# Bias tables kept once in DRAM and read with reversed keys, and a residual rescaled by VectorE: a change to a two-block transformer kernel

## The chip, the cores and the metric

The kernel runs on one core of a Trainium2 chip. A core has a TensorE (matmul; its weight loads are listed apart as PEld), a VectorE (DVE), a ScalarE (ACT), a GpSimd (POOL) and a SyncE (SP), which here only issues DMAs. All DMAs of the core, from SP's queue and from GpSimd's, run on the same 16 DMA engines. The metric is the device time of one execution in microseconds; lower is better.

## What is computed

One sequence of 256 tokens with 2048 features goes through two transformer blocks in fp32. Cut to what matters here:

```python
# block 1: NSA attention (16 heads, 4 key groups) and a SwiGLU feed-forward
h = x + nsa_mixer(rmsnorm(x, mix_norm_g), rel_bias, ...)
h = h + swiglu(rmsnorm(h, ffn_norm_g), ffn_w_in, ffn_w_out)
x = rmsnorm(h, final_norm_g)

# block 2: modulation from c, two attentions side by side, a squared-ReLU feed-forward
mod = silu(c) @ w_mod + b_mod            # six vectors of 2048
h = rmsnorm(x, attn_norm_g) * (1 + sc1) + sh1
proj = h @ w_in
o_a = swa_sink_attention(q_a, k_a, v_a, sinks, rel_bias_2)   # 16 heads, window of 128
o_b = mla_attention(q_nope, q_rope, k_nope, k_rope, v_b)     # 8 heads
x = x + g1 * (concat(o_a, o_b) @ w_out)
h = rmsnorm(x, mlp_norm_g) * (1 + sc2) + sh2
x = x + g2 * (relu(h @ w_ff1) ** 2 @ w_ff2)
out = rmsnorm(x, final_norm_g_2)
```

NSA and SWA add a relative bias to their scores: `bias[q, k] = rel_bias[bucket(q - k)]`, which depends only on the distance of query and key, and places outside the causal window are masked.

## The kernel before

**Products.** Activations lie feature-major, [128 features, 256 tokens]. A weight matrix streams through SBUF in pieces of 512 KB: SP's queue loads `raw` (5 buffers), ScalarE rounds it to a high part `whi` (line 84), VectorE subtracts for the low part `wlo` (line 85), each with 4 buffers, and TensorE makes three products of each tile (lines 127 to 129, or 163 to 165 where tokens are the output rows). So each piece of 512 KB gives TensorE 24 products of 256 columns.

**Order.** Each engine works through a queue of its own in order. The program is traced once, and a scheduler sets the order in each queue. Background work is spread over the products by `step`: in block 1 the stream over w_mod (`mod_columns`: GpSimd's queue loads 512 KB, line 705; VectorE multiplies and adds, line 711; after 16 loads TensorE sums over the lanes, line 692), and before it the loads for the compression of keys and values (line 479, GpSimd's queue, 256 KB each, two for each piece while the second key gemm runs). `after` holds such a load back until the last product traced before it. The compression's products (line 497) need `ku`, which VectorE makes (line 470) from `kc`, the evacuated key and value products (line 395).

**Bias.** `bias_table` makes a table [16 heads, 384 distances] on TensorE and VectorE (lines 354 and 356) and GpSimd's queue writes it to a DRAM scratch 128 times over, once for each of 128 query rows (line 358: 3 MB out of the 16 partitions of `btab`). It is called twice: for NSA at the start of `nsa`, for SWA ahead of the loop over the four NSA head groups. `bias_rows` (line 362) reads from it, each partition q from its own copy with an offset of one element more for each q, so that row q holds the biases of its 256 keys in ascending order. NSA does this once for each group of four heads (512 KB), SWA once for each pair of heads (256 KB), both with two buffers. `soft` then adds scores and bias, takes the row's extremum (line 540, VectorE), and ScalarE makes the exponentials (line 542).

**Block 2's attention** (`block2_attention`). `h` holds the input of block 1's last norm until the end of `qgroup(0)`. Then its square sums give `r1`, `r1s` holds `r1` on every partition, and GpSimd multiplies `h` in place by `r1s` and by `vecs["final"]`: four times two operations on [128, 4 x 256] (lines 816 and 817). Then come the MLA latents, and a loop: `mla_pair(2 * i)` and `swa(i)` for i in 0 to 3, with `qgroup(4)` after the first, then `swa(4)` to `swa(7)`. An MLA pair multiplies the queries up, applies the rope (`rope`, lines 899 to 903: a product with `swap`, then three VectorE operations, the last of which reads two tiles in SBUF), and then runs two heads (scores in lines 909 to 912). The next reader of `h` is the first evacuation of `mlp` (line 1034).

Of the kernel before, what the change touches and what calls it, by code (L numbers as in the profile page):

```python
# [17 lines left out]
S = 256  # L18
# [20 lines left out]
def constants():  # L39
    f = np.float32  # L40
    ident = np.eye(128, dtype=f)
    dist = 255 - np.arange(384)
# [24 lines left out]
class Kernel:  # L67
# [8 lines left out]
    # ---------------------------------------------------------------- helpers  # L76
# [19 lines left out]
    def load_w(self, pieces, kk, n):  # L96
        """pieces: (dest column, AP) ; returns the high and low part [128, kk, n]."""
        return self.split_w(self.load_raw(pieces, kk, n), kk, n)
# [16 lines left out]
    def raw_cols(self, w, ld, row, kk, cols):  # L115
        """cols: list of (first column, count)"""
        n = sum(c for _, c in cols)
        pieces, o = [], 0
        for c0, cn in cols:
            pieces.append((lambda t, o=o, cn=cn: t[:, :, o:o + cn],  # L120
                           self.src(w, row * ld + c0, [[ld, 128], [128 * ld, kk], [1, cn]])))
            o += cn
        return self.load_raw(pieces, kk, n)
# [7 lines left out]
    def gemm(self, w, ld, row, xs, cols, evac, kk=2, order=None):  # L131
        """out^T[cols, S] = w[row:, cols]^T x ; evac(i, bank) gets two output tiles a bank;
        order: that of the contraction, in pieces of kk"""
# [19 lines left out]
    def gemm_tok(self, w, ld, row, xs, cols, evac, kk=2, lag=0):  # L153
        """out[S, cols] = x^T w[row:, cols] ; evac(token tile, bank)
        lag: by how many pieces of the contraction the second token tile follows the first"""
# [36 lines left out]
    def step(self, units):  # L192
        """advances the background streams by the tensor engine's time (1: 16 x 512 weight rows/columns)"""
# [6 lines left out]
    def columns(self, specs, tag, queue=None):  # L200
        """specs: (AP of a vector, rows of 128) -> [128, rows] with one column for each row of 128"""
# [16 lines left out]
    def rstd_col(self, terms, eps, pool, name):  # L218
        """terms: list of ([128 features, S] AP, column [128,1]) whose weighted sum over features
        is the mean square; returns the column [128 tokens, 2] of 1/sqrt(mean + eps)."""  # L220
# [11 lines left out]
    def sqrt_table(self):  # L232
        """has the table of the square root loaded ahead of its use"""
        self.nc.scalar.activation(self.warm, self.sacc[:, 0:1], AF.Sqrt)

    def rsqrt(self, v, pool, name, n=2):
        """1/sqrt of a column, with a Newton step after the table's square root"""
# [10 lines left out]
    def replicate(self, col, n=2):  # L248
        """[128 tokens, 2] column -> psum [128, S], the same row on every partition"""
# [31 lines left out]
    # ---------------------------------------------------------------- start  # L281
    def start(self):
# [5 lines left out]
        # opens the tensor engine's clock gate while the first loads run  # L288
# [11 lines left out]
    def norm_x(self):  # L300
        """x into feature-major h, x * g split in parts; the sums of squares follow in self.inner"""
# [42 lines left out]
    # ---------------------------------------------------------------- NSA  # L344
    def bias_table(self, rel, which, pool):
        """table[h, 255 - dist] = -bias, masked places BIG, in a DRAM scratch once for each of 128 rows"""
# [10 lines left out]
        d = self.dram.tile([128, 16, 384], F32, name=f"bt{which}")  # L357
        nc.gpsimd.dma_start(d.rearrange("q h i -> h q i"), t[:, None, :].to_broadcast([16, 128, 384]))
        return d

    def bias_rows(self, d, h0, n, dst):
        self.nc.gpsimd.dma_start(dst, bass.AP(tensor=d.tensor, offset=d.offset + h0 * 384 + 127,
                                              ap=[[16 * 384 - 1, 128], [384, n], [1, 256]]))

    def nsa(self, xs, ssq, mp):
        nc, a, tc = self.nc, self.a, self.tc
        W, LD = a["nsa_w_in"], 5168
        with ExitStack() as es:
# [3 lines left out]
            # keys of a group: selected, window of the first token tile, compressed; the second tile's  # L372
# [92 lines left out]
    def blocks(self, ku, kc, pos, ci):  # L465
        """the overlapping blocks with their positions added, one row of the block after another"""
# [8 lines left out]
    def load_w1(self, j):  # L475
        """rows 256 (j // 2) .. of the first matrix of one of the compressions"""
# [13 lines left out]
    def compress(self, cp, ku, kT, vcc):  # L490
        """both compressions, side by side in two halves of the array's columns"""
# [42 lines left out]
    def soft(self, parts, sb, sums, sh=None):  # L534
        """parts: (psum slice, bias slice, columns of sb, mask column count): the scores and bias are
        negated; leaves exp(s - max) in sb and the sums in `sums`"""
# [8 lines left out]
    def nsa_head(self, w, hd, g, q, bt, kT, vt, vcc, gate):  # L545
# [6 lines left out]
        # first token tile, and the compressed scores of both  # L552
# [7 lines left out]
        self.soft([(s[:, 0:128], bt[:, 128:256], sl(0, 128)), (s[:, 128:256], bt[:, 128:256], sl(128, 256)),  # L560
                   (s[:, 256:263], bt[:, 159:256:16], sl(256, 263)),
                   (s[:, 272:287], bt[:, 31:256:16], sl(272, 287))], sb, sums)
# [12 lines left out]
        # second token tile  # L575
# [6 lines left out]
        self.soft([(s[:, 0:256], bt, sl(0, 256)), (s[:, 256:512], bt, sl(256, 512))], sb, sums)  # L582
# [9 lines left out]
        # weighted values of the three branches  # L592
# [11 lines left out]
    # ---------------------------------------------------------------- residual products  # L604
    def add_h(self, ms, n=2):
        """evacuation that adds a bank's n tiles into h; ms: first tile of the first bank"""
# [7 lines left out]
    def square_sums(self, scale=None):  # L614
        """a function that adds the squares of h[k], .. h[k + n - 1], and keeps those of the last call apart"""
# [21 lines left out]
    def scaled(self, k, g):  # L637
        """h[k] * g, split"""
# [7 lines left out]
    # ---------------------------------------------------------------- first FFN  # L646
# [35 lines left out]
    # ---------------------------------------------------------------- modulation vector  # L682
    def modulation(self, pool, segs):
        """steps that stream w_mod and leave silu(c) @ w_mod of the 1024-column segments in modv"""
# [15 lines left out]
    def mod_columns(self, pool, acc, s):  # L700
        """acc = the products of silu(c) with w_mod's columns of segment s, yet to be summed over lanes"""
# [12 lines left out]
    def after(self, ins):  # L714
        """paces a background load: not before the last product traced so far"""
# [9 lines left out]
    # ---------------------------------------------------------------- second block, attention  # L725
    def block2_attention(self, es, p, vecs, mod, mv):
        """h holds the input of block 1's last norm; returns the tiles of the mixed heads"""
# [4 lines left out]
        # norms of block 1's end and of the attention's input in one factor  # L732
        r12 = self.replicate(self.rstd_col(self.sums(self.cD[:, 0:1], 1), EPS * EPS, e, "r12c"))
        xs = self.modulated(e, r12, mod["g1"], mv[:, 0:16])
        # latents
# [71 lines left out]
        # x of block 2, in place  # L807
# [6 lines left out]
        for k in range(0, KT, 4):  # L814
            hs = self.h[:, k:k + 4, :]
            nc.gpsimd.tensor_tensor(hs, hs, r1s[:, None, :].to_broadcast([128, 4, S]), OP.mult)
            nc.gpsimd.tensor_tensor(hs, hs, vecs["final"][:, k:k + 4, None].to_broadcast([128, 4, S]), OP.mult)
        # MLA latents up
# [47 lines left out]
        def swa(hp):  # L866
            bt = p.tile([128, 2, 257], F32, name="bt2", tag="bt2", bufs=2)
            self.bias_rows(d2, 2 * hp, 2, bt[:, :, 0:256])
            nc.gpsimd.tensor_copy(bt[:, :, 256], self.nsink[:, 2 * hp:2 * hp + 2])
            mix[hp] = self.swa_pair(p, qa[hp], kd[:, hp // 4, :], va, hp // 4, bt)  # L870

        for i in range(4):
            mla_pair(2 * i)
            swa(i)
# [6 lines left out]
    def modulated(self, pool, r, g, sh):  # L881
        """h * r * g + sh, split; r: the factors of the tokens on every partition"""
# [49 lines left out]
    def swa_pair(self, p, q, kd, va, g, bt):  # L932
# [3 lines left out]
        for j in range(2):  # L936
# [7 lines left out]
            self.soft([(s[:, 0:257], bt[:, j, :], cs[0]), (s[:, 257:386], bt[:, j, 128:257], cs[1])], sb, sums)  # L944
# [17 lines left out]
    # ---------------------------------------------------------------- all  # L962
# [170 lines left out]
```

## Time and profile before

| | |
|---|---|
| median of 3 runs | 2213.34 us (2207.52, 2213.34, 2214.29) |
| profiled execution, span from the first to the last instruction | 2205.4 us (no other time of this execution is given) |
| TensorE busy | 2135.2 us, 97% |
| VectorE busy | 1460.0 us, 66% |
| ScalarE busy | 1017.8 us, 46% |
| GpSimd busy | 182.2 us, 8% |
| mean granted TensorE clock | 0.984 |
| read from and written to DRAM | 487.87 MB and 8.44 MB |

How to read it: the span is that of one execution taken by the hardware profiler. Matmuls are pipelined and their ends are modelled, so a busy TensorE isn't TensorE at its peak. Granted clock is the share of full speed that the throttle allowed. In views by line, "L85 DVE wlo<-raw,whi" is line 85 of the kernel on VectorE, which writes the tile wlo from raw and whi; an arrow behind an idle time names what ended it. Views of one stretch ("56.80:92.00") give its length, then busy time and instruction count of TensorE, its weight loads, VectorE, ScalarE and GpSimd, then granted clock, DMA share and GB/s. All times are counted from the span's start.

### The profile page before, as it was taken

The page shows a single profiled execution, that of the slowest core. Times are in us where ns is not written, and L with a number is a line of the kernel's source. Part 1 is how long each engine was busy: PE and PEld are TensorE (multiplying, and loading weights), DVE is VectorE, ACT ScalarE, POOL GpSimd, SP SyncE. Part 2 cuts the span into 40 slices and gives each one's busy share as a digit, 9 for nine tenths or more (in the row PEclk, how much of TensorE's full clock was granted, in tenths as well). Part 3 has the DMA queues.
Part 4 walks back from the last instruction along what each step waited for, and adds up shares of the span by engine and source line. Part 5 has one row for each costly group of instructions (what it writes and reads, how often), then busy time and mean ns, then how long its engine had stood idle before and what let it go on. Part 6 is the DMA issues. An engine that isn't in the chain of part 4 may idle for free.

```text
span 2205.4 us, 40878 instructions
## 1 busy us (share of the span) xinstructions
PE 2135.2 (97%) x16359; PEld 2007.6 (91%) x16359; DVE 1460.0 (66%) x2113; ACT 1017.8 (46%) x1511; POOL 182.2 (8%) x321
## 2 busy tenths in 40 slices
PE   9799699999999999999999979999999999999998
PEld 8588599999999999999999978899989989988987
DVE  6356477687777777777776776567776555565555
ACT  5234356544444444443445545546534534543543
POOL 2301000000011010111010030000100000000000
PEclk9899899999999999999999999999999999999999
DMA  8969954588888888888976543367887666656754
GB/s 226 317 192 295 202 153 154 185 288 279 279 298 282 286 290 283 288 289 281 292 242 188 158 132 125 106 182 237 281 291 259 211 192 192 194 191 193 195 193 134
DMA packets 289455, 499.26 MB, mean 226 GB/s; under 512 B 22807, under 2 KB 138586, under 8 KB 289008
## 3 DMA queue, kind: packets, MB, share of 16 engines
q1 hardware_dynamic: 254480, 372.64, 53.4%
q0 software_dynamic: 34784, 124.01, 18.5%
q8 instruction: 128, 2.10, 0.4%
q14 instruction: 63, 0.52, 0.1%
HBM read 487.87 MB, written 8.44 MB: 225 GB/s over the span
## 4 chain that ended last, share of the span: by engine, by line
PE 91%; DMA 4%; DVE 2%; issue 2%; ACT 0%; POOL 0%; SPq 0%; ACTq 0%; DVEq 0%; POOLq 0%
PE acc L128 22%; PE acc L127 22%; PE acc L129 22%; PE acc L164 6%; PE acc L165 6%; PE acc L163 6%; DMA mw<-w_mod 3%; DMA raw<-nsa_w_in 1%; PE O L497 1%; DVE qr L903 1%; PE S L578 1%; DVE wlo L85 0%; PE S L939 0%; PE O L954 0%; PE O L597 0%
## 5 line engine op out<-in xcount | busy, mean ns | idle before, releaser
L84 ACT ACTIVATE whi<-raw 128x1024 fp32r<-128x1024 f32 (+1 forms) x710 | 746.6, 1052 | 975.1 <-PE acc L128 642.6
L85 DVE TENSOR_TENSOR wlo<-raw,whi 128x1024 fp32r<-128x1024 f32 (+1 forms) x710 | 854.3, 1210 | 414.3 <-ACT whi L84 400.3
L127 PE MATMUL acc<-x,whi 128*128 128x256 f32 x3200 | 889.7, 279 | 11.1 <-ACT whi L84 10.0
L128 PE MATMUL acc<-x,whi 128*128 128x256 f32 x3200 | 890.0, 279 | 0.0
L129 PE MATMUL acc<-x,wlo 128*128 128x256 f32 x3200 | 888.2, 278 | 1.6 <-DVE wlo L85 1.6
L127 PEld LDWEIGHTS acc<-x,whi 128*128 128x128 f32 x3200 | 602.7, 189 | 17.5 <-ACT whi L84 11.7
L128 PEld LDWEIGHTS acc<-x,whi 128*128 128x128 f32 x3200 | 604.3, 189 | 6.7 <-issue 5.8
L129 PEld LDWEIGHTS acc<-x,wlo 128*128 128x128 f32 x3200 | 603.7, 189 | 3.9 <-DVE wlo L85 2.3
L711 DVE SCALAR_TENSOR_TENSOR macc<-mw,csil,macc 128x1024 f32<-128x1024 f32 x180 | 231.0, 1283 | 210.8 <-DMA mw<-w_mod 210.2
L128 PE MATMUL acc<-u,whi 128*128 128x256 f32 x1260 | 352.3, 281 | 0.0
L129 PE MATMUL acc<-u,wlo 128*128 128x256 f32 x1260 | 350.1, 280 | 0.0
L127 PE MATMUL acc<-u,whi 128*128 128x256 f32 x1260 | 347.4, 280 | 1.6 <-DVE h L611 1.1
L128 PEld LDWEIGHTS acc<-u,whi 128*128 128x128 f32 x1260 | 237.4, 188 | 3.7 <-issue 2.3
L129 PEld LDWEIGHTS acc<-u,wlo 128*128 128x128 f32 x1260 | 238.3, 189 | 1.6 <-issue 0.5
L127 PEld LDWEIGHTS acc<-u,whi 128*128 128x128 f32 x1260 | 235.2, 189 | 3.2 <-issue 1.9
L164 PE MATMUL acc<-whi,u 128*128 128x512 f32 (+1 forms) x544 | 206.2, 379 | 0.0
L165 PE MATMUL acc<-wlo,u 128*128 128x512 f32 (+1 forms) x544 | 206.1, 379 | 0.0
L163 PE MATMUL acc<-whi,u 128*128 128x512 f32 (+1 forms) x544 | 204.4, 376 | 0.0
L705 POOL DMA_DIRECT2D mw<-w_mod x192 | 103.2, 538 | 959.3 <-PE acc L129 623.2
L164 PEld LDWEIGHTS acc<-whi,u 128*128 128x128 f32 x544 | 102.1, 188 | 20.6 <-issue 0.4
L163 PEld LDWEIGHTS acc<-whi,u 128*128 128x128 f32 x544 | 102.1, 188 | 20.3
L165 PEld LDWEIGHTS acc<-wlo,u 128*128 128x128 f32 x544 | 102.2, 188 | 18.4
(347 smaller groups left out, 1350.8 us busy)
## 6 DMA issues: line engine op xcount, KB each, us to landing
raw<-w_ff SPq DMA_DIRECT2D x256, 512.0 KB, 4.2
mw<-w_mod POOLq DMA_DIRECT2D x192, 512.0 KB, 5.9
raw<-ffn_w_in SPq DMA_DIRECT2D x352, 256.0 KB, 5.0
raw<-ffn_w_out SPq DMA_DIRECT2D x87, 512.0 KB, 5.2
raw<-nsa_w_in SPq DMA_DIRECT2D x82, 512.0 KB, 5.6
raw<-nsa_w_out SPq DMA_DIRECT2D x32, 512.0 KB, 4.6
raw<-w_out SPq DMA_DIRECT2D x32, 512.0 KB, 4.2
raw<-w_in SPq DMA_DIRECT2D x24, 512.0 KB, 4.0
```

The source lines that it names most:

```text
L84: self.nc.scalar.activation(hi, x, AF.Copy)
L85: self.nc.vector.tensor_tensor(lo, x, hi.bitcast(F32), OP.subtract)
L127: mm(out, wh, xh, start=first, stop=False, skip_group_check=True)
L128: mm(out, wh, xl, start=False, stop=False, skip_group_check=True)
L129: self.last = mm(out, wl, xh, start=False, stop=last, skip_group_check=True)
L163: mm(o, xt[:, 0, q], hi, start=k == 0, stop=False)
L164: mm(o, xt[:, 1, q], hi, start=False, stop=False)
L165: self.last = mm(o, xt[:, 0, q], lo, start=False, stop=k == nk - 1)
L497: nc.tensor.matmul(ph[64 * ci:64 * ci + 60, :S], ku[:, ci, 2 * n + i, :], self.w1[2 * n + ci][:, i, :], start=n + i == 0, stop=n == 15 and ...
L578: mm(s.rearrange("p (b t n) -> p t b n", t=2, n=128)[:, t], q1, kT[:, g, 272 * t:272 * t + 256].rearrange("p (b n) -> p b n", n=128), star ...
L705: ld = nc.gpsimd.dma_start(wt, self.src(self.a["w_mod_2"], k * 128 * LD + s * 1024, [[LD, 128], [1, 1024]]))
L711: nc.vector.scalar_tensor_tensor(acc, wt, csil[:, k:k + 1], acc, op0=OP.mult, op1=OP.add)
```

## The change

Three things change together.

1. `bias_table` writes its table once, [16, 384], 24 KB. So that all partitions can read from the one copy, the table is turned round: its column i stands for the distance i - 127 (before: 255 - i). Partition q starts q elements further in, and gets its 256 biases with the keys in descending order.
2. The reader goes backwards through them: `keys` builds an access pattern with a step of -1 (or -16 for the compressed keys) over the bias tile, and `soft` gets that in place of the plain slice. In SWA the sink's column moves from the end of the tile to its start.
3. The eight GpSimd operations on `h` leave. `rescale` does the same on VectorE, one operation for each of the 16 feature tiles (`h[k] * final[k] * r1s`), four of them after each of the first four MLA pairs.

```diff
 def constants():
-    dist = 255 - np.arange(384)
+    dist = np.arange(384) - 127
...
     def bias_table(self, rel, which, pool):
-        d = self.dram.tile([128, 16, 384], F32, name=f"bt{which}")
-        nc.gpsimd.dma_start(d.rearrange("q h i -> h q i"), t[:, None, :].to_broadcast([16, 128, 384]))
+        d = self.dram.tile([16, 384], F32, name=f"bt{which}")
+        nc.gpsimd.dma_start(d, t)
         return d

     def bias_rows(self, d, h0, n, dst):
-        self.nc.gpsimd.dma_start(dst, bass.AP(tensor=d.tensor, offset=d.offset + h0 * 384 + 127,
-                                              ap=[[16 * 384 - 1, 128], [384, n], [1, 256]]))
+        self.nc.gpsimd.dma_start(dst, bass.AP(tensor=d.tensor, offset=d.offset + h0 * 384,
+                                              ap=[[1, 128], [384, n], [1, 256]]))
+
+    def keys(self, t, first, last, step=1):
+        n = t.ap[-1][1]
+        return bass.AP(tensor=t.tensor, offset=t.offset + n - 1 - first,
+                       ap=[list(t.ap[0]), [-step, len(range(first, last, step))]])
...
     def nsa_head(...)
-        self.soft([(s[:, 0:128], bt[:, 128:256], sl(0, 128)), (s[:, 128:256], bt[:, 128:256], sl(128, 256)),
-                   (s[:, 256:263], bt[:, 159:256:16], sl(256, 263)),
-                   (s[:, 272:287], bt[:, 31:256:16], sl(272, 287))], sb, sums)
+        near, both = self.keys(bt, 128, 256), self.keys(bt, 0, 256)
+        self.soft([(s[:, 0:128], near, sl(0, 128)), (s[:, 128:256], near, sl(128, 256)),
+                   (s[:, 256:263], self.keys(bt, 159, 256, 16), sl(256, 263)),
+                   (s[:, 272:287], self.keys(bt, 31, 256, 16), sl(272, 287))], sb, sums)
...
-        self.soft([(s[:, 0:256], bt, sl(0, 256)), (s[:, 256:512], bt, sl(256, 512))], sb, sums)
+        self.soft([(s[:, 0:256], both, sl(0, 256)), (s[:, 256:512], both, sl(256, 512))], sb, sums)
...
     def block2_attention(...)
-        for k in range(0, KT, 4):
-            hs = self.h[:, k:k + 4, :]
-            nc.gpsimd.tensor_tensor(hs, hs, r1s[:, None, :].to_broadcast([128, 4, S]), OP.mult)
-            nc.gpsimd.tensor_tensor(hs, hs, vecs["final"][:, k:k + 4, None].to_broadcast([128, 4, S]), OP.mult)
+        def rescale(ks):
+            for k in ks:
+                nc.vector.scalar_tensor_tensor(self.h[:, k, :], self.h[:, k, :], vecs["final"][:, k:k + 1], r1s,
+                                               op0=OP.mult, op1=OP.mult)
...
         def swa(hp):
-            self.bias_rows(d2, 2 * hp, 2, bt[:, :, 0:256])
-            nc.gpsimd.tensor_copy(bt[:, :, 256], self.nsink[:, 2 * hp:2 * hp + 2])
+            self.bias_rows(d2, 2 * hp, 2, bt[:, :, 1:257])
+            nc.gpsimd.tensor_copy(bt[:, :, 0], self.nsink[:, 2 * hp:2 * hp + 2])
...
         for i in range(4):
             mla_pair(2 * i)
+            rescale(range(4 * i, 4 * i + 4))
             swa(i)
...
     def swa_pair(...)
-            self.soft([(s[:, 0:257], bt[:, j, :], cs[0]), (s[:, 257:386], bt[:, j, 128:257], cs[1])], sb, sums)
+            self.soft([(s[:, 0:257], self.keys(bt[:, j, :], 0, 257), cs[0]),
+                       (s[:, 257:386], self.keys(bt[:, j, :], 128, 257), cs[1])], sb, sums)
```

## The prediction

> **What bounds the kernel now.** I read the page first: how busy TensorE is, and the slices of its granted clock.
>
> ```profile
> span 2205.4 us, 40878 instructions
> PE 2135.2 (97%) x16359; PEld 2007.6 (91%) x16359; DVE 1460.0 (66%) x2113; ACT 1017.8 (46%) x1511; POOL 182.2 (8%) x321
> PEclk9899899999999999999999999999999999999999
> ```
>
> TensorE is the bound: busy for 97% of the span. So a change gains only where TensorE stands still or runs at a reduced clock. Second I took TensorE's own waits, longest first.
>
> ```profile
> PE S L692 <- DVE macc L711: 21.8, 2, 21.5
> PE S L910 <- DVE qr L903: 12.0, 1, 12.0
> PE acc L127 <- ACT whi L84: 10.0, 2, 9.7
> PE O L497 <- DVE ku L470: 4.1, 1, 4.1
> ```
>
> Four waits hold 47.9 us of all that TensorE waits for, and three of them are single events of 9.7 to 21.5 us. Third I asked for the stretches around them (and one normal stretch beside each): time, TensorE busy with its instruction count, then weight loads, VectorE, ScalarE, GpSimd, granted clock, DMA share, GB/s.
>
> ```profile
> 20.00:54.00 34.00, 34.00 (x285) 33.03 (x284) 25.77 (x44) 15.78 (x22) 6.08 (x8) 1.00 0.88 177
> 56.80:92.00 35.20, 19.53 (x116) 15.39 (x115) 14.61 (x24) 10.40 (x11) 9.89 (x14) 0.76 1.02 312
> 70.00:80.00 10.00, 8.97 (x59) 7.95 (x59) 2.45 (x2) 3.04 (x3) 6.41 (x9) 0.84 1.03 409
> 220.00:230.00 10.00, 10.00 (x91) 10.00 (x90) 4.37 (x5) 2.13 (x2) 0.55 (x1) 1.00 1.00 129
> 232.00:258.00 26.00, 4.48 (x26) 3.20 (x25) 5.34 (x8) 3.17 (x3) 0.53 (x1) 0.61 0.97 211
> 1312.00:1334.00 22.00, 9.98 (x39) 7.49 (x38) 16.16 (x17) 4.04 (x11) 11.82 (x6) 0.61 0.15 47
> 1340.00:1350.00 10.00, 10.00 (x70) 8.64 (x69) 9.57 (x25) 6.04 (x14) 0.95 (x2) 1.00 0.72 227
> ```
>
> In each of the three the clock is reduced as well (0.76, 0.61, 0.61): after an idle stretch TensorE also works on slowly for some microseconds. What is lost is therefore counted by instructions: length of the stretch less its instructions at the normal rate.
>
> **Part 1, the tables in DRAM (two writes of 3 MB become two of 24 KB).** The DMA list (size, median us to landing), then what follows the first write in time:
>
> ```profile
> bt<-btab POOLq DMA_DIRECT2D x2, 3072.0 KB, 35.5
> mw<-w_mod POOLq DMA_DIRECT2D x192, 512.0 KB, 5.9
> 34.99 1.06 POOL L358 DMA_DIRECT2D bt<-btab  x1 [22.91 <-DVE btab L356]
> 47.83 31.15 DMA raw<-nsa_w_in
> 65.49 1.06 ACT L84 ACTIVATE whi<-raw 128x1024 fp32r<-128x1024 f32 x1 [18.95 <-DMA raw<-nsa_w_in]
> 66.60 0.58 PE L127 MATMUL acc<-x,whi 128*128 128x256 f32 x1 [9.74 <-ACT whi L84]
> 81.40 1.03 DVE kc L395 x2
> 86.74 5.35 PE O L497 x30
> ```
>
> Issued at 34.99, the write holds the DMA engines until about 70 (34.99 + 35.5). Weights behind it come late (ScalarE waits 18.95 us for one piece), TensorE lives off its loaded pieces until 56.86 and then stops for 9.74 us. From 70 on, with the write landed, the same engines move 409 GB/s. The 4.1 us wait for ku is a child of the same delay: the chain goes from the late piece (until 78.98) over its split to VectorE's evacuation of kc (81.40).
>
> Loss of this place: in 35.2 us TensorE did 116 instructions. At the 0.119 us of the stretch just before (34.0 / 285) to the 0.143 us of 1340 to 1350 (10 / 70) these are 13.8 to 16.6 us; most are products of the weights' kind, so I take 14.6: 20.6 us lost. Not all goes. From the evacuation (81.40) to the first product that needs the last ku (86.74) are 5.3 us of VectorE's own work, which stays, and TensorE has little to do beside it; of the 4.1 us of wait I leave 2. Term: 18.6; bounds 9.7 (the first wait alone) and 20.6.
>
> The small write needs a cover check for what is issued next to it: while TensorE works on the second key gemm, each piece of 24 products (24 x 0.119 = 2.86 us) takes 512 KB of weights and GpSimd's queue issues two loads of 256 KB for the compression, 1.05 MB in 2.86 us, 367 GB/s. That is under the 409 of the row, but not far under (rival A).
>
> The second write, at 214.38:
>
> ```profile
> 214.38 1.06 POOL L358 DMA_DIRECT2D bt<-btab  x1 [5.44 <-issue]
> 215.44 37.06 DMA mw<-w_mod
> 249.26 1.06 ACT L84 ACTIVATE whi<-raw 128x1024 fp32r<-128x1024 f32 x1 [11.25 <-DMA raw<-nsa_w_in]
> ```
>
> A load of w_mod issued right behind it takes 37.06 us, against 5.9 for the median. TensorE's queue has the sum over w_mod (L692) next, which needs it: the 21.5 us wait. The weights are late too (11.25 us at ScalarE), so without the L692 wait TensorE would still have stood; with the write gone both reasons go. Loss: 26.0 less 26 x 0.110 = 23.1 us. What is late next: the load would land near 221.3 (215.44 + 5.9), some ten microseconds before TensorE gets to it (at about 232, where the stretch begins). Term 23.1; bounds 21.5 and 23.1.
>
> Reading the tables (12 loads): number of rows, 1 KB each, and bytes stay; only their source shrinks from 3 MB to 24 KB that all 128 partitions read with an overlap. The trace has loads whose 128 rows read the same few KB:
>
> ```profile
> bt<-bt POOLq DMA_DIRECT2D x4, 512.0 KB, 5.7
> z<-b_mod POOLq DMA_DIRECT2D x4, 256.0 KB, 4.3
> bt<-bt POOLq DMA_DIRECT2D x8, 256.0 KB, 3.7
> ```
>
> 4.3 us against 3.7 at the same size: 0.6 us more for each of the 12 at worst, and they are issued a head group or a pair ahead of their use. Cost 0; if that lead were gone, 12 x 0.6 = 7 us. A gain there is worth nothing, as no one waits for these loads now.
>
> **Part 2, the keys reversed.** VectorE's score-and-bias operation (L540) reads the bias with step -1 (and -16). Columns: a head of NSA 128 + 128 + 7 + 15 + 256 + 256 = 790, 16 heads, 12,640; SWA 16 x 386 = 6,176; together 18,816. No row shows a negative step. The nearest are the positive step of 16 against step 1:
>
> ```profile
> L540 DVE CUSTOM_DVE_ANT_0 sb<-S,bt 128x256 f32<-128x256 f32 x32 | 12.2, 419 | 0.3 <-PE S L578 0.2
> L540 DVE CUSTOM_DVE_ANT_0 sb<-S,bt 128x128 f32<-128x128 f32 x32 | 8.5, 283 | 1.1 <-PE PT L571 0.8 <-PE S L555 0.3
> L540 DVE CUSTOM_DVE_ANT_0 sb<-S,bt 128x15 f32<-128x15 f32 x16 | 2.7, 170 | 0.0
> L540 DVE CUSTOM_DVE_ANT_0 sb<-S,bt 128x7 f32<-128x7 f32 x16 | 2.6, 160 | 0.0
> 256.00:430.00 174.00, 173.78 (x1284) 159.18 (x1282) 126.13 (x437) 99.48 (x291) 13.87 (x36) 1.00 0.56 172
> 1324.00:1440.00 116.00, 114.61 (x737) 95.07 (x737) 66.77 (x222) 61.73 (x159) 5.54 (x12) 0.96 0.35 113
> ```
>
> Step 1: (419 - 283) / 128 = 1.06 ns a column. Step 16: (170 - 160) / 8 = 1.25. So between 0 and 0.19 ns a column, 0 to 3.6 us of VectorE in all. It lies beside TensorE's work: in the NSA heads (256 to 430) VectorE has 47.9 us idle and TensorE waits 0.2. I take 0, since the step of 16, further from step 1 than a reversal, is already nearly free; with the cover gone 3.6.
>
> [...]
>
> **Part 3, the rescale of h.** Eight GpSimd operations leave, 16 on VectorE come, four behind each MLA pair.
>
> ```profile
> 1307.10 9.32 POOL L816 TENSOR_TENSOR h<-h,r1s 128x1024 f32<-128x1024 f32 x4
> 1316.38 7.44 POOL L817 TENSOR_TENSOR h<-h,vec 128x1024 f32<-128x1024 f32 x4
> 1309.12 14.98 DVE L903 TENSOR_TENSOR qr<-qr,rt 128x256 f32<-128x256 f32 x1
> 1344.05 0.42 DVE L903 TENSOR_TENSOR qr<-qr,rt 128x256 f32<-128x256 f32 x1
> L888 DVE SCALAR_TENSOR_TENSOR tx<-h,gm,S x16: 470/475/481, 1211.3 to 1226.1; 128x256 f32<-128x256 f32 x16
> ```
>
> One VectorE operation of the rope takes 14.98 us in place of 0.42. It starts while GpSimd works (1307.10 to 1323.82) and ends 0.3 us after it: it was locked out for that time. TensorE's score product needs its result: the 12.0 us wait. With no GpSimd operation left there, 14.6 us of VectorE go. Loss at TensorE: 22.0 less 39 instructions at 0.143 = 16.4 us, clock included. Bounds 12.0 and 16.4; I take 16.4, because the slow clock follows from the idle time.
>
> The 16 new operations are like L888 (same form, [128, 256] times a column times a tile): 16 x 0.475 = 7.6 us. VectorE is idle for 49.2 of the 116 us in which they fall, with TensorE at 114.6 of 116. A group of four (1.9 us) can stand ahead of a softmax step in VectorE's queue; the queue behind it holds the splits and the scores of the next SWA pair, and TensorE waits for those once it has used its weights up. Cost between 0 and 7.6; I take 2, near the covered end. On GpSimd's queue the loads of the next bias rows (L362) no longer have the rescale before them, which no one waited for. The first reader of the new h (L1034) stands in program order behind all SWA pairs, so behind the last group.
>
> **Sum.** 18.6 + 23.1 + 16.4 - 2 = 56.1 us off the span of 2205.4: 2149.3. The page gives no time of this execution but its span; the median of the runs, 2213.34, lies 7.9 above it, taken as unchanged. 2213.3 - 56.1 = 2157.2, so 2158.
>
> **Rivals.**
> A: the first gap closes only in part. Freed from the table, the compression's loads meet the weights (367 GB/s wanted); if the engines give 300, eight pieces take 3.5 us in place of 2.86, 5 us more, and the ku wait stays at 4.1 with its slow clock. Term 10 instead of 18.6: 2167. Against it: 409 GB/s in the row, and 21.9 us of loaded work at 34.99.
> B: VectorE becomes what TensorE waits for between the MLA pairs; all 7.6 us and some of the reversal (3.6) are exposed: 9 us more, 2167. For it: 9.57 of 10 busy in 1340 to 1350. Against: 57% over the whole stretch.
> C, on the other side: the reversed operand falls to a slow path. It decides from where it fills VectorE's idle time in the NSA heads and eats the gain: (47.9 + 58) / 12,640 = 8.4 ns a column over the 1.06. At 10 ns, 78 us exposed there and some 20 in SWA: 2253. Against: 0.19 ns for step 16.
> D: the reversal costs 0.19 ns or more a column where it is not covered (the last four SWA pairs, few weights left): 2160 to 2162. [...]
> E: the new lengths make the scheduler put TensorE's queue in another order, and a new wait takes half of a gap's gain: 10 to 20 us, 2168 to 2178.
>
> **How the numbers follow.** Forecast as summed: 0.66. A 0.09, B 0.07, D 0.07, E 0.08, C 0.02, and 0.01 that the writes were not the cause and nothing changes. 2158 is the likeliest case. The range 2147 to 2176 holds the forecast, A, B, D and most of E, with some microseconds for the time outside the span; it leaves out C, the rest of E and a gain above 66 us, and the forecast's own is 2149 to 2164. 0.3% is 6.6 us, about what a measurement of this kernel can tell from no change: all but C and the last case gain more, so faster 0.96, same 0.02, slower 0.02.
>
> **What would show it.** Right: no TensorE wait above 3 us from 40 to 260 and in the rope; DMA share near 1 with 130 GB/s gone after the table writes; clock 1.00 through the NSA heads' start; every L903 at 0.42; L540 at 419 and 283 ns; 16 operations of 0.475 us on VectorE. Wrong: TensorE waiting for ACT whi or ku before 100 (A), for VectorE between 1310 and 1400 (B), L540 longer (C, D), a wait at a place that has none now (E).

## The result, and the profile after

| | before | after |
|---|---|---|
| median | 2210.43 us (2206.92 to 2214.29, 4 runs) | 2147.46 us (2146.03 to 2148.10, 4 runs) |
| ratio | | 0.9717, 95% interval 0.9695 to 0.9739 |
| span of the profiled execution | 2205.4 us | 2145.4 us |
| mean granted clock | 0.984 | 0.997 |
| written to DRAM | 8.44 MB | 2.20 MB |

The changed kernel is 2.8% faster: 63.0 us by the medians, 60.0 us by the two profiled spans. The forecast was 2158 with a range from 2147 to 2176, so the time lies half a microsecond inside its lower edge, and outside the 2149 to 2164 that the prediction gave for the case that it took as likeliest. One run of the kernel with the first unread write alone (below) fell into a slower state, 2366.92 us at a granted clock of 0.847, and is left out of its figures. The kernels of the experiments ran on three chips, on which the kernel before had medians of 2209.81, 2211.85 and 2207.91 us; their times stand beside 2147.46 where a difference to the changed kernel is given.

The page after, its first lines, then TensorE's longest waits (total, how many, longest):

```profile
span 2145.4 us, 40875 instructions
PE 2120.9 (99%) x16359; PEld 1999.3 (93%) x16359; DVE 1450.2 (68%) x2129; ACT 1018.8 (47%) x1511; POOL 164.5 (8%) x313
PEclk9999999999999999999999999999999999999999
PE PT L317 <- DMA xt<-x: 2.7, 1, 2.7
PE S L253 <- DVE r12c L245: 1.6, 1, 1.6
PE S L561 <- DVE nm L547: 1.6, 1, 1.6
```

All four waits of before are gone, the one for `ku` too, and no new one stands in their place (the load of `xt`, at the start of the kernel, cost 2.8 before). The granted clock shows no slice under 0.9 any more.

Where the time came from is read at three landmarks that both kernels pass: TensorE's transposes of the gates (behind the key, value and compression products), VectorE's first and last update of `h` in block 1, and its first update of `h` in the MLP. Rows by tile: count, ns min/median/max, first to last start. Before:

```profile
L430 PE MATMUL S<-ident,gt x2: 273/273/273, 200.8 to 200.9; 128*128 128x128 f32 x2
L611 DVE TENSOR_TENSOR h<-h,acc x41: 422/680/689, 430.4 to 1206.2; 128x512 f32<-128x512 f32 x39, 128x256 f32<-128x256 f32 x2
L1034 DVE SCALAR_TENSOR_TENSOR h<-acc,modc,h x16: 469/473/485, 1443.0 to 1488.4; 128x256 f32<-128x256 f32 x16
```

After:

```profile
L437 PE MATMUL S<-ident,gt x2: 273/273/273, 177.3 to 177.4; 128*128 128x128 f32 x2
L619 DVE TENSOR_TENSOR h<-h,acc x41: 416/682/690, 385.4 to 1159.9; 128x512 f32<-128x512 f32 x39, 128x256 f32<-128x256 f32 x2
L1045 DVE SCALAR_TENSOR_TENSOR h<-acc,modc,h x16: 474/477/485, 1382.0 to 1427.3; 128x256 f32<-128x256 f32 x16
```

| stretch | before | after | gain | term forecast |
|---|---|---|---|---|
| start to the gates (first table write) | 200.8 | 177.3 | 23.5 | 18.6 |
| gates to the first h (second table write) | 229.6 | 208.1 | 21.5 | 23.1 |
| first to last h of block 1 (untouched) | 775.8 | 774.5 | 1.3 | 0 |
| last h to the MLP's first h (rope, rescale) | 236.8 | 222.1 | 14.7 | 14.4 |

The untouched stretch measures the noise of such a reading: over all kernels below it lay between 772.4 and 778.9 us.

The first gap in windows (columns as in the prediction): the changed kernel's place of the first gap, and what follows up to the gates; then the same following part of before.

```profile
57.30:71.50 14.20, 14.20 (x114) 11.72 (x113) 11.15 (x22) 7.24 (x8) 6.76 (x10) 1.00 0.86 316
71.50:177.30 105.80, 105.80 (x717) 91.22 (x716) 57.41 (x57) 38.31 (x39) 14.22 (x24) 1.00 0.78 259
```

```profile
92.00:200.80 108.80, 108.80 (x712) 91.71 (x712) 57.15 (x59) 38.30 (x39) 14.81 (x25) 1.00 0.76 251
```

Before, 116 instructions took 35.2 us (the prediction's row); now 114 take 14.2. That is 21.0 of the 23.5 us. The rest lies behind the gap: 105.8 us for 717 instructions against 108.8 for 712, 3.0 us less, with TensorE busy throughout in both; the whole stretch starts 0.5 us later. What made that part slower before was not tried.

The rescale and the rope after it, VectorE in order of time; then the reversed reads by shape; then the DMAs (size, median us to landing):

```profile
1260.26 4.04 DVE L825 SCALAR_TENSOR_TENSOR h<-h,vec,r1s 128x256 f32<-128x256 f32 x10
1265.42 2.07 DVE L825 SCALAR_TENSOR_TENSOR h<-h,vec,r1s 128x256 f32<-128x256 f32 x5
1269.07 0.42 DVE L913 TENSOR_TENSOR qr<-qr,rt 128x256 f32<-128x256 f32 x1
L547 DVE CUSTOM_DVE_ANT_0 sb<-S,bt 128x256 f32<-128x256 f32 x32 | 12.2, 420 | 0.0
L547 DVE CUSTOM_DVE_ANT_0 sb<-S,bt 128x128 f32<-128x128 f32 x32 | 8.4, 285 | 6.8 <-PE PT L579 3.7 <-PE S L562 3.0
L547 DVE CUSTOM_DVE_ANT_0 sb<-S,bt 128x15 f32<-128x15 f32 x16 | 2.8, 172 | 0.0
L547 DVE CUSTOM_DVE_ANT_0 sb<-S,bt 128x7 f32<-128x7 f32 x16 | 2.6, 161 | 0.0
bt<-btab POOLq DMA_DIRECT2D x2, 24.0 KB, 5.0
bt<-bt POOLq DMA_DIRECT2D x4, 512.0 KB, 5.3
bt<-bt POOLq DMA_DIRECT2D x8, 256.0 KB, 4.4
```

The last rope operation is back at 0.42 us. The 16 rescale operations (the lines show 15, one more stands alone at 1264.55) do not stand between the MLA pairs at all: the scheduler put them in one burst from 1260.26 to 1267.49, with two other operations in between, ahead of that last rope operation.

### The profile page after: what moved, and what is told of

The parts are those of the page before. It is cut to its first block, busy times and chain, and to the rows that moved or that the text cites. A ratio compares the mean times of both kernels' runs of the same rounds, so it can differ in the third digit from the quotient of the medians.

```text
span 2145.4 us, 40875 instructions
## 1 busy us (share of the span) xinstructions
PE 2120.9 (99%) x16359; PEld 1999.3 (93%) x16359; DVE 1450.2 (68%) x2129; ACT 1018.8 (47%) x1511; POOL 164.5 (8%) x313
## 3 DMA queue, kind: packets, MB, share of 16 engines
q0 software_dynamic: 33440, 117.76, 16.4%
## 4 chain that ended last, share of the span: by engine, by line
PE 93%; DMA 3%; issue 2%; DVE 2%; ACT 1%; POOL 0%; SPq 0%; ACTq 0%; DVEq 0%; POOLq 0%
PE acc L127 23%; PE acc L128 23%; PE acc L129 22%; PE acc L164 6%; PE acc L165 6%; PE acc L163 6%; DMA mw<-w_mod 2%; PE O L504 1%; DVE wlo L85 1%; PE S L586 1%; DMA g2r<-modv 0%; PE S L949 0%; PE O L605 0%; PE O L965 0%; PE S L561 0%
## 5 line engine op out<-in xcount | busy, mean ns | idle before, releaser
L85 DVE TENSOR_TENSOR wlo<-raw,whi 128x1024 fp32r<-128x1024 f32 (+1 forms) x710 | 855.0, 1211 | 397.8 <-ACT whi L84 385.3
L164 PEld LDWEIGHTS acc<-whi,u 128*128 128x128 f32 x544 | 102.2, 188 | 20.6 <-issue 0.4
```

What stands on the lines that cost most here:

```text
L85: self.nc.vector.tensor_tensor(lo, x, hi.bitcast(F32), OP.subtract)
L164: mm(o, xt[:, 1, q], hi, start=False, stop=False)
```

## Experiments

**The parts alone.** The changed tables with the rescale of before, and the rescale of the change in the kernel before:

```diff
# tables only (against the changed kernel)
-        def rescale(ks): ...            # 16 VectorE operations, 4 behind each MLA pair
+        for k in range(0, KT, 4): ...   # 8 GpSimd operations, ahead of the MLA latents
```

> The changed kernel with the eight GpSimd operations on h put back in their old place; tables and reversed keys stay. Theory (three separate gaps): the two gaps of the tables stay closed and the rope's gap comes back: 45 us less than before (the gain up to the first h of block 1 was 45.0 us in the traces), so a ratio of about 0.980, and one VectorE operation of the rope takes some 15 us again. Rival (the parts work only together, since the gap at the rope came from the order of the queues): the rope's gap doesn't come back, 58 to 60 us less.

> The kernel before with the rescale on VectorE alone; tables as before. Theory: only the rope's gap closes: 14 to 15 us less than before, ratio about 0.9935, both stalls behind the table writes stay at 9.7 and 21.5 us on TensorE. Rival (VectorE's 7.6 us come onto the path when the tables' part doesn't shift the queues): less than 9 us.

Tables only: 2159.99 us (2158.04 to 2161.86), ratio to before 0.9762 [0.9723, 0.98]. Rescale only: 2193.41 us (2190.71 to 2195.5), 0.9907 [0.9872, 0.9942]. 49.8 and 16.4 us add up to 66.2, where both together bring 63. By the profiled spans (2159.5 and 2191.6 against 2205.4) it is 45.9 and 13.8, together 59.7, where both bring 60.0. So the two parts are nearly independent, and the theory held (45 for the first, 14 to 15 for the second). Tables only, TensorE's longest wait, VectorE's last rope operation and GpSimd beside it:

```profile
PE S L919 <- DVE qr L912: 12.0, 1, 12.0
1258.92 14.97 DVE L912 TENSOR_TENSOR qr<-qr,rt 128x256 f32<-128x256 f32 x1
1256.89 9.31 POOL L825 TENSOR_TENSOR h<-h,r1s 128x1024 f32<-128x1024 f32 x4
1266.17 7.43 POOL L826 TENSOR_TENSOR h<-h,vec 128x1024 f32<-128x1024 f32 x4
```

Rescale only keeps the other three waits:

```profile
PE S L692 <- DVE macc L711: 21.5, 1, 21.5
PE acc L127 <- ACT whi L84: 10.4, 2, 9.4
PE O L497 <- DVE ku L470: 4.1, 1, 4.1
```

**Is it the writes' time on the DMA engines?** The small tables stay, and a write that nobody reads is added right behind each of them (the last of the four expectations says "ahead"; in the runs the table's own 24 KB are issued first, 0.5 to 2.1 us earlier): two of 3 MB, the first of the two alone, two of 1.5 MB, two of 0.75 MB.

```diff
     def bias_table(self, rel, which, pool):
...
         d = self.dram.tile([16, 384], F32, name=f"bt{which}")
         nc.gpsimd.dma_start(d, t)
+        x = self.dram.tile([128, 16, 384], F32, name=f"bx{which}")      # 64 and 32 for the smaller ones
+        nc.gpsimd.dma_start(x.rearrange("q h i -> h q i"), t[:, None, :].to_broadcast([16, 128, 384]))
         return d
```

> The changed kernel plus the two writes of 3 MB as they were, into a scratch that nothing reads; small tables, reversed keys and the VectorE rescale stay. Theory (the writes occupy the DMA engines, and weights queue behind them): both gaps come back in full, 43 to 46 us more than the changed kernel, so like the kernel with the rescale alone. Rival (the gaps came from work that waited for the tables themselves, or from reading them): nothing comes back, under 3 us.

> As the kernel with both unread writes, but only the first one. Theory: only the first gap comes back, 21 to 24 us more than the changed kernel (23.5 in the traces, of which 21.0 in the stretch of the wait itself). Rival (the forecast's own split, where some of the ku wait stays in any case): 18.6 us. If the second gap's place reacts too, the two are not separate.

> The changed kernel plus two unread writes of half the size (64 copies, 1.5 MB each). Theory (TensorE has about 20 us of loaded work at each write, 21.9 us at the first and 18.0 at the second, and a half write holds the DMA engines for about 17.7): nearly nothing comes back, 0 to 6 us more than the changed kernel, TensorE's two waits under 2 us. Rival (each MB written costs TensorE the same): half of the 42 us that the full unread writes cost, 21 us.

> The changed kernel with two unread writes of 0.75 MB ahead of the table writes (32 copies; the earlier runs had 128 and 64). Theory (a write blocks the DMA engines for its whole time, and a delay is repaid only by the small rate that the weights leave over, so the loss goes with the write's time): landing 10 to 11.5 us each; from the two earlier sizes, at the first place 21.2 us for 35.5 and 10.9 for 19.4, 0.64 us a us from 2.4 us up, gives 5 us to the gates; at the second place 7.3 for 19.4 and about 19 for 35.5 give 0 to 1; in all 2147.5 + 5 to 6 = 2152 to 2154. Rival (loaded pieces, 21.9 us of TensorE's work, cover any write shorter than that, and the loss of the 1.5 MB write came from just exceeding it): no loss at either place, no TensorE wait above 3 us, 2146 to 2149.

| unread writes | time | ratio to before | gates | first h |
|---|---|---|---|---|
| none (the changed kernel) | 2147.46 | 0.9717 [0.9695, 0.9739] | 177.3 | 385.4 |
| two of 0.75 MB | 2152.24 (2148.47 to 2163.44) | 0.9740 [0.9692, 0.9787] | 177.1 | 386.6 |
| two of 1.5 MB | 2163.64 (2162.53 to 2164.76) | 0.9772 [0.9735, 0.9809] | 188.2 | 403.6 |
| the first of 3 MB | 2169.80 (2165.69 to 2175.07) | 0.9808 [0.9759, 0.9857] | 198.5 | 405.4 |
| two of 3 MB | 2189.53 (2185.29 to 2206.12) | 0.9922 [0.9875, 0.9969] | 199.4 | 424.9 |

With two unread writes of 3 MB the waits are back, although no one waits for the data:

```profile
PE S L702 <- DVE macc L721: 18.9, 1, 18.9
PE acc L127 <- ACT whi L84: 11.4, 2, 9.8
```

So most of the loss comes with the writes themselves, without any change to the reading, the layout or the addresses. 42 us were lost, and 43 to 46 expected; in the traces it is 22.1 us up to the gates and 17.4 from there to the first h, of 23.5 and 21.5. What the other 5.5 us were isn't shown. The first write alone brings back the first gap (21.2 us at the gates) and not the second.

One rival stays untested: the write stands in GpSimd's own queue, and that queue is held up too. A wait of the kernel before:

```profile
POOL w L479 <- DMA bt<-btab: 20.8, 1, 20.8
```

Behind the write GpSimd issues seven loads for the compression (40.20 to 48.68); the next goes out only at 70.19, released by the write. The load of w_mod that TensorE waits 21.5 us for stands behind the second write in the same queue. That the shared engines are held up as well is shown by the weights, which come over SP's queue and are late at both places (18.95 and 11.25 us at ScalarE). How much of the second gap goes with the one and how much with the other is open, for no run has the write on another queue.

The smaller sizes show how the cost grows. My expectation for 1.5 MB held neither way: 0 to 6 us by the theory, 21 by the rival, 16.2 measured. The first wait for weights was covered as the theory had it (1.7 us), but not the waits that come after it. What I had left out is what piles up behind the write. DMAs, chain, windows and two TensorE waits of that kernel:

```profile
bx<-btab POOLq DMA_DIRECT2D x2, 1536.0 KB, 19.4
48.95 19.91 DMA raw<-nsa_w_in
46.00:51.00 5.00, 5.00 (x45) 5.00 (x44) 4.06 (x6) 1.06 (x1) 2.12 (x3) 1.00 0.93 91
56.00:61.00 5.00, 2.54 (x20) 2.13 (x19) 1.23 (x1) 1.06 (x1) 2.42 (x4) 1.00 1.03 406
61.00:66.00 5.00, 5.00 (x30) 5.00 (x31) 1.23 (x1) 1.63 (x2) 2.27 (x5) 0.66 1.04 409
66.00:71.00 5.00, 5.00 (x40) 4.30 (x38) 2.17 (x2) 1.56 (x2) 1.30 (x2) 1.00 1.04 408
PE S L702 <- DVE macc L721: 7.1, 2, 6.5
PE O L506 <- DVE ku L479: 4.5, 1, 4.5
```

The write is over near 56, but a load issued at 48.95 still takes 19.91 us, and the engines run at 406 to 409 GB/s for 15 us more (the highest seen in a 5 us window of these kernels is 414). Behind that TensorE stops for the `ku` that comes late (4.5 us, up to 75.50), and at the second write for the sum over w_mod. The changed kernel moves 391 GB/s in the same 5 us:

```profile
56.00:61.00 5.00, 5.00 (x45) 5.00 (x44) 3.38 (x4) 1.77 (x2) 2.15 (x4) 1.00 1.02 391
```

Of the five windows from 46 to 71, with 330, 346, 391, 365 and 214 GB/s, that is the tightest; windows that lie otherwise show up to 409 (60 to 65). By the rates of the five some 20 GB/s are spare in the tightest window and 45 to 80 in the full ones beside it, an estimate, so a debt is paid back only over several windows. The 0.75 MB write then told whether the loss goes straight with the write's time (5 us at the gates, my theory, from a line through the two sizes) or whether loaded pieces cover a short one (0, the rival). The kernel of 0.75 MB:

```profile
bx<-btab POOLq DMA_DIRECT2D x2, 768.0 KB, 10.8
56.00:61.00 5.00, 5.00 (x45) 5.00 (x44) 2.58 (x3) 2.04 (x3) 2.16 (x4) 1.00 1.04 411
ACT whi L84 <- DMA raw<-nsa_w_in: 7.8, 4, 2.7
PE S L702 <- DVE macc L721: 2.9, 1, 2.9
```

The gates come at 177.1, as without any write. ScalarE waits 7.8 us for four pieces, and TensorE works through it without a break. My theory fell at the first place: the loss there sets in somewhere between 0.75 and 1.5 MB. The rival's bound falls as well, since a write of 19.4 us, shorter than the 21.9 us of loaded work, cost 10.9. At the second place something small is lost: the first h comes at 386.6, 1.2 us behind the latest of the kernels without an unread write (383.4 to 385.4), and TensorE waits 2.9 us for the sum over w_mod, where the changed kernel waits 1.0. The median of 2152.24 fits the theory's total, but the four runs spread over 15 us, and in the traced execution, 2150.26, the two places account for 1.2 us.

**What the rescale costs on VectorE.** Without the 16 operations (`h` is then not rescaled, which changes the output), and with each of them held back by `after`, so that they spread over the MLA pairs:

```diff
-            rescale(range(4 * i, 4 * i + 4))                                   # left out
...
-                nc.vector.scalar_tensor_tensor(self.h[:, k, :], ...)           # held back
+                self.after(nc.vector.scalar_tensor_tensor(self.h[:, k, :], ...))
```

> The changed kernel with the 16 VectorE operations left out, so that h isn't rescaled. Theory (they are covered altogether, since the trace has all 16 in one run of 7 us behind r1s while TensorE has products): the stretch from the last h of block 1 to the first of the MLP stays at 222.1 us within 1, time 2146 to 2148. Rival 1 (the 2 us of the forecast): 220, 2145. Rival 2 (all exposed): 214.5, 2140.

> The changed kernel with each of the 16 VectorE operations held back until the last weight product of its MLA pair, so that they really stand between the pairs, four by four. Theory (VectorE has 40% idle there and TensorE has products): the same time as the changed kernel within 2 us, 2146 to 2150. Rival (a group ahead of a softmax step delays TensorE): up to 7.6 us more, 2155.

Left out: 2146.68 us (2141.64 to 2152.99); last h to the MLP's h takes 221.7 us. The seven kernels that have the 16 operations in one burst lie between 221.2 and 222.4 there, so the 7.6 us of VectorE work are covered and no cost is seen. Held back: 2153.56 us (2146.64 to 2157.21), 224.0 us in that stretch; the operations run in groups of four from 1258.5 to 1285.8, where the last rope operations of the four pairs run from 1262.0 to 1319.8, so they lie among the first pairs only. The median lies outside the 2146 to 2150 of the theory and near the rival's 2155, and 224.0 lies above the spread of the burst. But the ratios to before, 0.9723 [0.9681, 0.9764] and 0.9717 for the change, don't tell the two apart, and the traced execution was the quickest of the four. Nothing is gained by pacing the operations; whether it costs some microseconds is open.

**How long GpSimd locks VectorE out.** The tables of the change with only the first four of the eight GpSimd operations (the product with `final_norm_g` is left out), and with all eight, two behind each of the first four MLA pairs, held back by `after`:

```diff
         for k in range(0, KT, 4): # four
             nc.gpsimd.tensor_tensor(hs, hs, r1s..., OP.mult)
-            nc.gpsimd.tensor_tensor(hs, hs, vecs["final"]..., OP.mult)
...
-                nc.vector.scalar_tensor_tensor(...)                            # paced
+            self.after(nc.gpsimd.tensor_tensor(hs, hs, r1s..., OP.mult))
+            nc.gpsimd.tensor_tensor(hs, hs, vecs["final"]..., OP.mult)
```

> The kernel with the tables alone (rescale on GpSimd at its old place), with only the first four of the eight GpSimd operations: the product with the norm's weights is left out. Theory (VectorE's operation with two inputs in SBUF stays locked out until GpSimd's whole run of operations is over, not just the one it meets): the rope's operation takes 14.97 - 7.43 = 7.5 us, TensorE waits 4 to 5 us, 7 to 9 us less than with all eight (2160.0). Rival (it is let in at the end of the operation that it meets): under 2.9 us, no wait on TensorE; all eight would then have shown 2.4 as well.

> The changed kernel with the rescale back on GpSimd, but two operations behind each of the first four MLA pairs, each pair held back until what was traced before it, so never eight in a run. Theory (VectorE's operation on two SBUF inputs is locked out for a whole back-to-back run of GpSimd's, and only for that): no operation of VectorE takes more than 9.3 + 7.4 = 16.7 us; where one of them meets a pair of GpSimd operations it is held for what is left of the pair, 4 to 16 us, and 0 to 4 such meetings occur; with about 8 us of lost TensorE time for a meeting in the middle of a pair, 2147 to 2175, 2158 as the middle. Rival (what cost time before was only the place, right ahead of the first rope): spread out, the GpSimd operations cost nothing, 2145 to 2150, and no VectorE operation of the rope or of the splits is above 1 us.

Four operations: 2156.69 us (2149.26 to 2160.39), 229.6 us in the stretch, where the eight of the tables-only kernel took 235.9. TensorE waits 4.6 us for the rope, as expected; the time is 3.3 us less than with eight by the medians and 6.3 in the stretch, where 7 to 9 were expected.

```profile
1262.50 9.32 POOL L825 TENSOR_TENSOR h<-h,r1s 128x1024 f32<-128x1024 f32 x4
1264.53 7.59 DVE L911 TENSOR_TENSOR qr<-qr,rt 128x256 f32<-128x256 f32 x1
```

VectorE's operation ends at 1272.12, 0.3 us after GpSimd's fourth (1271.82). A lock given up at the end of each instruction would have let it in near 1264.8, where the first of the four ends (1262.50 + 9.32 / 4). So the rope's operation is shut out over all four GpSimd instructions here (7.59 us in place of 0.42), and over all eight in the tables-only kernel (14.97 us), not over one alone.

Paced: 2157.62 us (2153.92 to 2158.13), 233.1 us in the stretch; 10 us slower than the change (and every run slower than those of the forward-read kernel below, 2144.82 to 2153.46, which ran on the same chip), near the middle that was expected, though by more and shorter holds than I had expected (1.2 to 3.8 us each). In order of time GpSimd and then VectorE in that kernel, and a window over the place; behind it the changed kernel's window, which begins as long after the last h of block 1 (98.4 us):

```profile
1282.01 1.90 POOL L827 TENSOR_TENSOR h<-h,vec 128x1024 f32<-128x1024 f32 x1
1283.86 2.35 POOL L826 TENSOR_TENSOR h<-h,r1s 128x1024 f32<-128x1024 f32 x1
1286.29 2.77 POOL L827 TENSOR_TENSOR h<-h,vec 128x1024 f32<-128x1024 f32 x1
1276.46 2.66 DVE L959 TENSOR_SCALAR sb<-sb,sums 128x256 f32<-128x256 f32 x2
1282.33 4.97 DVE L85 TENSOR_TENSOR wlo<-raw,whi 128x1024 fp32r<-128x1024 f32 x1
1287.22 2.11 DVE L914 TENSOR_TENSOR qr<-qr,rt 128x256 f32<-128x256 f32 x1
1255.00:1290.00 35.00, 28.40 (x203) 25.45 (x201) 28.46 (x48) 15.51 (x34) 21.09 (x14) 0.99 0.41 133
```

```profile
1258.30:1293.30 35.00, 33.76 (x241) 29.42 (x240) 28.13 (x82) 17.35 (x40) 3.01 (x6) 1.00 0.52 165
```

The split (L85) normally takes 1.21 us. It starts at 1282.33, is held through the first two GpSimd operations, which follow each other without a gap (1283.86 against 1283.91), and ends 1.1 us after the second (1286.21). The third reads what the second wrote, so it starts 0.08 us later, and in that gap VectorE gets in; the third then takes 2.77 us in place of 1.9. So an expectation of mine is to be narrowed: the lock lasts, in these traces, as long as GpSimd's operations follow without a gap. Operations with two input tiles are not the only ones held: the two of L959, with one input tile and a column, take 2.66 us in place of 0.54 while GpSimd works (a multiplication by r1s from 1276.30 to 1278.78). In 35 us TensorE does 203 instructions where the changed kernel does 241: 38 at 0.140 (33.76 / 241) are 5.3 of the 11 us lost. The rest lies behind. The mean granted clock of the whole execution is 0.995 against 0.997.

**The reversed read by itself.** The bias read forward, so that the biases meet the wrong keys; all else as in the change.

```diff
     def keys(self, t, first, last, step=1):
-        return bass.AP(tensor=t.tensor, offset=t.offset + n - 1 - first,
-                       ap=[list(t.ap[0]), [-step, len(range(first, last, step))]])
+        return bass.AP(tensor=t.tensor, offset=t.offset + first,
+                       ap=[list(t.ap[0]), [step, len(range(first, last, step))]])
```

> The changed kernel with one edit: the bias tile is read forward (step +1 and +16) in place of backward, so each row's biases meet the wrong keys; instructions, sizes and order stay. Theory (the reversal is free): the score-and-bias operation keeps 420 ns for 256 columns, 285 for 128, 172 and 161 for 15 and 7, within 3 ns each, and the kernel stays within 5 us of the changed one (2142 to 2152). Rival (a step of -1 or -16 costs VectorE something): the four shapes get shorter by more than 3 ns, 0.19 ns a column or more, which is 48 ns at 256 columns, and the kernel gets 0 to 4 us faster.

2146.88 us (2144.82 to 2153.46). The operations take the same time forward as backward:

```profile
L546 DVE CUSTOM_DVE_ANT_0 sb<-S,bt 128x256 f32<-128x256 f32 x32 | 12.2, 420 | 0.0
L546 DVE CUSTOM_DVE_ANT_0 sb<-S,bt 128x15 f32<-128x15 f32 x16 | 2.8, 172 | 0.0
```

## Why the prediction was right, point by point

- **The bound and the reading of the gaps: right.** TensorE's four waits, and the slow clock around them, were the places where time was to be had; nearly all of the gain lies in the three stretches that hold them (23.5 + 21.5 + 14.7 = 59.7, against 60.0 us of span).
- **First table write: right in mechanism, too small by 4.9 us.** The term was 18.6 and its bound 20.6. Two steps failed. I left 2 us for the wait for `ku`, as "VectorE's own work, which stays": with `kc` made on time no wait for `ku` is left at all, and with the 1.5 MB writes, where the wait for weights is only 1.7 us, it is 4.5: it comes with the late pieces. And I counted the loss only in the stretch of the gap, up to 92; another 3.0 us came from the compression behind it, outside my bound.
- **Second table write: right.** 21.5 against 23.1, at the lower bound. The load of w_mod is not late any more; TensorE's wait for that sum is 1.0 us in place of 21.5. The unread write brought it back at 18.9. The gain fell 1.6 us short of the term; whether the engines or GpSimd's queue delayed that load is open (see above).
- **The cover for the small write (rival A): did not come, and the margin is thin for a short time only.** The changed kernel moves 391 GB/s in the tightest of the five windows there (409 from 60 to 65), near the highest rate seen, 414. The unread writes show what it means: 0.75 MB more at that place are free, 1.5 MB cost 10.9 us up to the gates.
- **Reading the small table: right, hidden.** 4.4 us for 256 KB, against 3.7 before; 512 KB 5.3 against 5.7. TensorE waits for none of it.
- **The reversal: right, 0** (rivals C and D out). 420 against 419 ns, 285 against 283, and the forward kernel is the same. (420 - 285) / 128 = 1.05 ns a column for a step of -1 here, where the step of 1 took (419 - 283) / 128 = 1.06.
- **The rope: right in mechanism; that the number fits is luck.** 14.7 against 16.4 - 2 = 14.4. Both halves were too large by about 2 and cancel: no cost of the rescale is seen where 2 were put, so the gap's own gain was some 14 to 15 rather than 16.4. The tables-only kernel agrees: 235.9 against 222.1 us, 13.8. Why counting instructions gave too much here isn't shown.
- **Rival B (VectorE becomes the bound): out.** With all 16 operations left out the stretch takes 221.7 us, within the 221.2 to 222.4 of the kernels that have them.
- **Rival E (the scheduler's order): no cost.** It was VectorE's order that changed, where the rival had TensorE's (which was not compared): the four groups became one burst ahead of the end of the first rope. No wait came of it, and spreading them brought nothing.
- **The sum.** 56.1 forecast, 60.0 by the spans. The last step, from span to time, was a slip: I added 7.9 us, the distance of one execution's span to the median of other executions. Around the span lie 1.8 us in each run (2147.21 for a span of 2145.4 here). 2205.4 - 56.1 + 1.8 would have given 2151.1, 3.6 above the measured time; so most of the 10.5 us between 2158 and 2147.46 is this step. It and the first term, too small by 4.9, err the same way, the second term by 1.6 the other way. That the time still fell into the range, by 0.46 us, owes as much to the range's width as to the sum.

## What to carry to other kernels

A DMA that replicates data for convenience was paid for here in the time that it holds the shared engines (two unread writes of 3 MB, 35.5 us each, cost 42 us): look up what is queued behind it, how many microseconds of loaded work the bound engine has (21.9 at the first write), and how far the steady rate lies under the highest rate seen (391 to 409 against 414 GB/s here), for by my estimate that margin is what pays the debt back. Moving work from GpSimd to a busier VectorE gained 13.8 us of the span by itself here, where GpSimd's operations read SBUF beside VectorE's two-input operation on the critical chain (14.98 us in place of 0.42). Convert a span into a time by what lies around the span in one and the same execution, never by another run's median.

## What the runs showed of the hardware

- GpSimd operations on SBUF that follow without a gap shut out a VectorE operation with two SBUF inputs for the whole of what is left of the run: 14.97 us with eight operations, 7.59 with four, in place of 0.42. Two operations with one input tile and a column were held too (2.66 us in place of 0.54). With GpSimd's operations paced, a gap of 0.08 us, from one that reads what the one before wrote, was enough to let VectorE in.
- A write of 3 MB out of 16 partitions lands after 35.5 us, 1.5 MB after 19.4, 0.75 MB after 10.8. Meanwhile the DMA engines are taken for more than 0.9 of their time and move 91 to 157 GB/s in all (windows of 5 us inside these writes).
- The cost of such a write is not in proportion to it, in this kernel with 21.9 us of loaded work ahead of TensorE: 0, 10.9 and 21.2 us up to the gates for 0.75, 1.5 and 3 MB.
